# Storing the first attention's queries in 2 KB runs, and taking a tile of 32 queries as every fourth column

## The chip, the core and the metric

The kernel runs on one core of one Trainium2 chip, as one launch. Times are device microseconds (us) of that core. The work is spread over TensorE (PE in the profile; its weight loads are PEld), VectorE (DVE), ScalarE (ACT), GpSimd (POOL), the issuing queue of SyncE (SP) and 16 DMA engines. Lower is better.

## What is computed

One encoder layer over 2048 tokens with 1024 features, in float32. Cut to what matters here:

```python
h  = rms_norm(x) * norm_mix
q_a, k_a, v_a, q_b, k_b, v_b, g_a, g_b = split(h @ w_in)     # 512 128 128 512 512 512 1024 1024
y_a = windowed_gqa(q_a, k_a, v_a, sink)      # 8 query heads in 2 groups of 4, 64 wide, one K and V per group
y_b = neighborhood_attn(q_b, k_b, v_b, rpb)  # 8 heads on a 32 x 64 grid of tokens
x  = x + (sigmoid(g_a + b) * (y_a @ w_proj_a) + sigmoid(g_b + b) * (y_b @ w_proj_b)) @ w_out
x  = x + relu(rms_norm(x) @ w_up) ** 2 @ w_down
out = rms_norm(x) * norm_final

# windowed_gqa, for a block of 128 queries and the 384 keys around it
sc = (q . k) * 64 ** -0.5 - slope[head] * |t - s|      # only where |t - s| <= 128
p  = softmax over the keys and one more logit, sink[head]
y  = p @ v
```

## The kernel before

**Precision.** Every operand of a large product is held as a high part (rounded to the format that TensorE reads in one pass) and a low part (the remainder); the product is three matmuls, high x high, high x low and low x high. So each result that becomes an operand again is written twice: ScalarE writes the high part, VectorE the low one.

**Stages.** First stage (about the first 360 us): the input projection for token blocks 0 and 1 (512 tokens each), and for most columns in a scheme with seven products in place of eight (`in_quad`, in the order 1, 2, 5, 6, 7, 4, 3). Its results go through `in_result`. Then the kernel runs the first attention (`attn_a`, 32 units: 2 head groups by 16 blocks of 128 tokens, about 360 to 615 us), and between its instructions, as filler, the same projection for token blocks 2 and 3 (`qk_tile`, `v_tile`, `gate_tile`). The second attention follows with more filler, then the output projection, and the two layers of the feed-forward part, which take the larger half of the time.

**Where queries come from.** A slice is one tile of 128 features (two heads) by one block of 512 tokens. `qk_parts` writes a slice's high and low parts side by side into a tile `t2` and returns the pairs of places for the DMAs that store it in DRAM. The query columns are `O_QA` to `O_KA`: four tiles of features, four blocks, 16 slices. The store is `qs_a[g][m]`, for head group `g` and half `m` of the tokens; its 128 rows are the 64 high and 64 low features of a head. Eight slices are made in the first stage (tile `ze`, a ring of two buffers, stored at L468), eight during the attention (tile `z`, a ring of three, stored at L709). The lines in question before: L446 (ScalarE) and L447 (VectorE) write the two parts with the scale 1/8 applied. The key and query tiles of the second attention take the other branch, L442 and L443, in which key tiles are written in steps of four words and query tiles in reversed runs of adjacent words.

**How `attn_a` uses them.** A unit loads its queries with one DMA (L774) into a tile `qa` with three buffers. It works in four steps of 32 tokens: the 32 queries of four heads are the 128 columns of the stationary operand (L784), and the 288 keys around them are the moving operand, in two matmuls (the high and low keys against the high and low queries, then crosswise). Before, a step's 128 columns are adjacent in the tile:

```python
PE.matmul(ps[:, :n], q[:, u].rearrange("p h q -> p (h q)"), ka[:, z, base + lo : base + hi], ...)
```

VectorE adds the bias of the distances and takes the row maximum (L786), ScalarE makes the exponentials (L788 to L791), GpSimd divides (L795), TensorE transposes (L802), the transposed part is split by ScalarE and VectorE (L805, L806), and two matmuls a chunk make the output (L807, L808); L813 and L814 evict it.

**Order.** Nothing in the code fixes the order of all instructions: a planner places them, engine by engine, by its own costs, with a few bounds written out by hand (`issue_after`). SP issues nearly all DMAs in one queue, in order; ScalarE issues a few.

Of the kernel before, what the change touches and what calls it, by code (L numbers as in the profile page):

```python
# [8 lines left out]
F32 = mybir.dt.float32  # L9
F32R = mybir.dt.float32r  # L10
AF = mybir.ActivationFunctionType
ALU = mybir.AluOpType
# [10 lines left out]
P = 128  # L23
KC = D // P
NB = 4
BT = 512
# [4 lines left out]
A_Q = 32  # L31
# [3 lines left out]
O_QA, O_KA, O_VA, O_QB, O_KB, O_VB, O_GA, O_GB = 0, 512, 640, 768, 1280, 1792, 2304, 3328  # L35
# [60 lines left out]
def encoder_layer(ctx, tc, x, norm_mix, w_in, b_gate, sink, rpb, w_pa, w_pb, w_out,  # L96
                  norm_mlp, w_up, w_down, norm_final, dist_a, mask_b, out):
    nc = tc.nc
    V, A, G, PE, SY = nc.vector, nc.scalar, nc.gpsimd, nc.tensor, nc.sync
# [16 lines left out]
    dp = pool("dp", space=DRAM)  # L116
# [10 lines left out]
    def T(pl, shape, dt, tag, bufs):  # L127
        n_t[0] += 1
        pl = pl[tag] if isinstance(pl, dict) else pl
        return pl.tile(shape, dt, tag=tag, bufs=bufs, name=f"{tag}_{n_t[0]}")  # L130
# [20 lines left out]

    qs_a = [[dp.tile([P, 32, 4, A_Q], F32, name=f"qs_a{g}{m}") for m in range(2)] for g in range(2)]
    ks_a = [dp.tile([2, P, S // 2], F32, name=f"ks_a{m}") for m in range(2)]
    vs_a = [dp.tile([2, P, 8, P], F32, name=f"vs_a{m}") for m in range(2)]
    qs_b = [dp.tile([2, P, 4, 4, P], F32, name=f"qs_b{t}") for t in range(4)]
# [225 lines left out]
    last_part, last_low = [None], [None]  # L383
# [45 lines left out]
    def qk_parts(col, b, src, t2):  # L429

        th, tl = t2[:, 0], t2[:, 1]
        if O_QB <= col < O_VB:
            if col < O_KB:

                pv = src.rearrange("p (r j c) -> p j r c", r=8, j=4)
                hv, hr, lr = (flipped(t) for t in (th, th.bitcast(F32R), tl.bitcast(F32R)))
            else:

                pv = src.rearrange("p (q r x) -> p q r x", q=2, r=4)
                hv, hr, lr = (t.rearrange("p (q x r) -> p q r x", q=2, r=4)  # L440
                              for t in (th, th.bitcast(F32R), tl.bitcast(F32R)))
            A.copy(hr, pv)  # L442
            V.tensor_tensor(out=lr, in0=pv, in1=hv, op=ALU.subtract)  # L443
        else:
            scale = 1.0 if col == O_KA else 0.125
            A.activation(th.bitcast(F32R), src, AF.Copy, scale=scale)  # L446
            last_low[0] = V.scalar_tensor_tensor(out=tl.bitcast(F32R), in0=src, scalar=scale, in1=th,  # L447
                                                 op0=ALU.mult, op1=ALU.subtract).ins
        parts = [(e, t2[e * 64 : e * 64 + 64]) for e in range(2)]
        if col < O_KA:  # L450
            dst, h = qs_a[col // 256][b // 2], col // P % 2 * 2
            n = BT // A_Q
            dst = dst.rearrange("(z p) u h q -> p z u h q", z=2)[:, :, b % 2 * n : (b % 2 + 1) * n]
            return [(dst[:, z, :, h + e], t[:, z].rearrange("p (u q) -> p u q", u=n)) for e, t in parts for z in range(2)]
        if O_QB <= col < O_KB:
            dst = qs_b[(col - O_QB) // P]
            return [(dst[e].rearrange("(z p) b j q -> p z b (j q)", z=2)[:, :, b], t) for e, t in parts]
        dst, o = (ks_a[b // 2], b % 2 * BT) if col == O_KA else (ks_b[(col - O_KB) // P], b * BT)
        return [(dst[e].rearrange("(z p) t -> p z t", z=2)[:, :, o : o + BT], t) for e, t in parts]
# [90 lines left out]
    for k in range(KC):  # L550
        ps = zbank(*tbanks[k % 6])
        turned(ps, tiles[0], k)
        h, l = (t[:, k % 4] for t in right[1 + k // 4])
# [142 lines left out]
    h_pages(2)  # L696


    def qk_tile(col, scale, tiled=False):
        raw = load_slice([(cols(w_in[0], col), KC)])  # L700
        yield
        hl = split_slice(raw, V if col == O_KA else G)
        yield
        for b in (2, 3):
            ps = psum("mm", 2)
            feature_tile(ps, hl, hp[b])
            out = qk_parts(col, b, ps, T(wp, [P, 2, BT], F32, "z", 3))
            for dst, t in out:
                SY.dma_start(dst, t)  # L709
            yield  # L710

    def v_tile(col):
        raw = load_slice([(cols(w_in[0], col), KC)])
        yield
        hl = split_slice(raw, V if col == O_VA else G)
        yield
        for b in (2, 3):
            ps = psum("mm", 2)
            feature_tile(ps, hl, hp[b])
            vt = T(wp, [P, 2, BT], F32, "z", 3)[:, 0]  # L720
            A.copy(vt, ps)
            out = v_parts(col, b, vt, psum("mm", 2), T(wp, [P, 2, BT], F32, "z", 3).rearrange("p a b -> p (a b)"))
            for dst, t in out:
                SY.dma_start(dst, t)
            yield
# [3 lines left out]
    SY.dma_start(dist, dist_a)  # L729
    bias_a = [None] * 2  # L730

    by_head = T(ap_, [P, 4], F32, "byhead", 1)
    slope, sink_p = by_head[:, 0:2], by_head[:, 2:4]
    for h in range(4):
        at = slice(h * A_Q, (h + 1) * A_Q)
        for g in range(2):
            G.memset(slope[at, g : g + 1], 2.0 ** -(4 * g + h + 1))
        G.tensor_copy(out=sink_p[at], in_=sink_t[at].rearrange("p (g h) -> p g h", g=2)[:, :, h])

    def make_bias_a(g):  # L740
        t = T(ap_, [P, A_K], F32, f"biasa{g}", 1)
# [23 lines left out]
    def attn_a(g, i):  # L765
        c0, c1 = (1 if i == 0 else 0), (2 if i == 15 else 3)
        if bias_a[g] is None:

            with tc.issue_after(shares[2]):
                make_bias_a(g)  # L770
        base = (i - 1) * P
        q = T(ap_, [P, 4, 4, A_Q], F32R, "qa", 3)
        s = sas[len(began) % 4]
        began.append(SY.dma_start(q.bitcast(F32), qs_a[g][i // 8][:, i % 8 * 4 : i % 8 * 4 + 4]).ins)  # L774
        ka, v = kas[g], vas[g]
        st = T(ap_, [P, 8, 4], F32, "sta", 8)
        mx, nm, sm, es, ri = (st[:, k, :] for k in range(5))
        sink_g = sink_p[:, g : g + 1]
        span = [(max(u * A_Q, c0 * P), min(u * A_Q + A_K, c1 * P)) for u in range(4)]
        for u, (lo, hi) in enumerate(span):  # L780
            n = hi - lo
            ps = psum("s", 3)
            for z in range(2):
                PE.matmul(ps[:, :n], q[:, u].rearrange("p h q -> p (h q)"), ka[:, z, base + lo : base + hi],  # L784
                          start=z == 0, stop=z == 1)
            V.tensor_tensor_reduce(out=s[:, u, lo:hi], in0=ps[:, :n], in1=bias_a[g][:, lo - u * A_Q : hi - u * A_Q],  # L786
                                   scale=1.0, scalar=sink_g, op0=ALU.add, op1=ALU.max, accum_out=mx[:, u : u + 1])
        A.activation(nm, mx, AF.Copy, scale=-1.0)  # L788
        A.activation(es, mx, AF.Exp, bias=sink_g, scale=-1.0)
        for u, (lo, hi) in enumerate(span):  # L790
            A.activation(s[:, u, lo:hi], s[:, u, lo:hi], AF.Exp, bias=nm[:, u : u + 1], accum_out=sm[:, u : u + 1])  # L791
        V.tensor_tensor(out=sm, in0=sm, in1=es, op=ALU.add)
        V.reciprocal(ri, sm)
        for u, (lo, hi) in enumerate(span):
            share = G.tensor_scalar(s[:, u, lo:hi], s[:, u, lo:hi], ri[:, u : u + 1], 1.0, ALU.mult, ALU.mult)  # L795
        shares.append(share.ins)
        yield
        po = psum("av", 1)
        for c in range(c0, c1):
            pt = psum("pt", 2)  # L800
            for u in range(4):
                PE.transpose(pt[:, u * P : (u + 1) * P], s[:, u, c * P : (c + 1) * P], ident)  # L802
            ph = T(ap_, [P, 512], F32R, "ph", 3)
            pl = T(ap_, [P, 512], F32R, "pl", 3)
            A.copy(ph, pt)  # L805
            V.tensor_tensor(out=pl, in0=pt, in1=ph.bitcast(F32), op=ALU.subtract)  # L806
            PE.matmul(po, v[:, i - 1 + c, :], ph, start=c == c0, stop=False)  # L807
            last = PE.matmul(po, v[:, i - 1 + c, :], pl, start=False, stop=c == c1 - 1).ins  # L808
        done.append(last)
        t = T(ap_, [64, 512], F32, "ya", 2)  # L810
        t4 = t.rearrange("d (h u q) -> d h u q", h=4, u=4)
        by_u = po.rearrange("p (u h q) -> p h u q", u=4, h=4)
        A.copy(t4, by_u[64:128])  # L813
        V.tensor_tensor(out=t4, in0=by_u[0:64], in1=t4, op=ALU.add)  # L814
        flush(queue=SY)
        put(y_a[g].rearrange("(h d) t -> d h t", d=64)[:, :, i * P : (i + 1) * P],
            t.rearrange("d (h q) -> d h q", h=4))
# [38 lines left out]
            yield  # L856


    dense = [qk_tile(O_KA, 1.0), v_tile(O_VA)]
    dense += [qk_tile(O_QA + t * P, 0.125) for t in range(4)]  # L860
    for t in range(4):
        dense.append(qk_tile(O_KB + t * P, 0.125))
        dense.append(qk_tile(O_QB + t * P, 1.0, tiled=True))
        dense.append(v_tile(O_VB + t * P))
    dense += [gate_tile(f, (2, 3)) for f in range(16)]
    for n in (0, 0, 1):
# [789 lines left out]
```

## Time and profile before

| | |
|---|---|
| median of three runs | 2615.67 us (2615.21 to 2619.52) |
| the profiled execution | 2615.13 us |
| its span, first to last instruction | 2613.4 us |
| TensorE busy | 2575.6 us, 99% |
| VectorE, ScalarE, GpSimd busy | 1604.9, 1230.9, 348.2 us |
| DMA queue of SP | 396416 packets, 470.99 MB, 57.9% of the 16 engines' span |
| mean granted TensorE clock | 0.998 |

How to read it: a profile is one execution. Busy times are unions of an engine's instructions; matmuls overlap each other in them, since their ends are modelled. In the view of stretches each row is one window of the span (its start and end, its length, then for each engine the busy time and the number of instructions, the granted clock of TensorE, the share of the DMA engines' time and GB/s). In the timeline a row is the start, the length, the engine, the line, the operation, its output and inputs and its count, with the idle time before it and what ended it in brackets. In the list of waits a row is the waiting instruction, what it waited for, the total in us, how often, and the longest. In the groups a row ends with the busy time, the mean length of one in ns, and the idle time of the engine before these instructions.

### The profile page before, as it was taken

The numbers are of one execution on the slowest core, as the hardware profiler recorded it, in microseconds if no ns is written. First come the engines' busy times: TensorE is split into PE (matmuls) and PEld (weight loads), VectorE is DVE, ScalarE is ACT, GpSimd is POOL, SyncE is SP. The second block draws the span as 40 slices with busy tenths as digits, with TensorE's granted clock in tenths as the row PEclk, the third lists the DMA queues.
The fourth block names the chain that finished last, engine by engine and source line by source line (L and its number), as shares of the span: only waits on it lengthen the run. The fifth ranks groups of instructions, "written<-read, shape, count | busy, mean of one in ns | idle before, by whom it ended". The sixth has DMA issues, their size and how long they took to land.

```text
span 2613.4 us, 34714 instructions
## 1 busy us (share of the span) xinstructions
PE 2575.6 (99%) x12140; PEld 2147.1 (82%) x12140; DVE 1604.9 (61%) x2621; ACT 1230.9 (47%) x2261; POOL 348.2 (13%) x461
## 2 busy tenths in 40 slices
PE   7999999999999999999999999999999999999999
PEld 6788788878888888888888888888888888888887
DVE  8776566655544444765578677766656535554766
ACT  5244346665555555633335544644444322322454
POOL 1000113334555551000001000100000000000010
PEclk9999999999999999999999999999999999999999
DMA  6767376565876745964556755854428825445555
GB/s 185 184 167 204 123 247 172 123 181 136 223 219 184 201 144 162 304 191 150 168 191 203 242 211 199 308 185 149 153 97 308 299 97 185 145 146 169 185 193 171
DMA packets 403647, 490.26 MB, mean 188 GB/s; under 512 B 94840, under 2 KB 238328, under 8 KB 401296
## 3 DMA queue, kind: packets, MB, share of 16 engines
q1 hardware_dynamic: 396416, 470.99, 57.9%
q10 hardware_dynamic: 7056, 17.04, 1.8%
q8 instruction: 96, 1.57, 0.2%
q14 instruction: 79, 0.65, 0.1%
HBM read 328.49 MB, written 159.45 MB: 187 GB/s over the span
## 4 chain that ended last, share of the span: by engine, by line
PE 87%; DVE 5%; DMA 3%; ACT 2%; issue 1%; SPq 1%; POOL 0%; DVEq 0%; POOLq 0%; ACTq 0%
PE b L300 15%; PE b L302 15%; PE b L301 15%; PE mm L205 6%; PE mm L203 6%; PE mm L204 6%; PE pt L203 2%; PE pt L204 2%; PE pt L205 2%; PE zb L302 2%; PE av L987 2%; PE zb L300 2%; PE zb L301 2%; PE pt L975 2%; PE s L947 2%; PE pt L802 1%
## 5 line engine op out<-in xcount | busy, mean ns | idle before, releaser
L301 PE MATMUL b<-dwh,dah 128*128 128x512 f32 x896 | 348.5, 389 | 0.0
L302 PE MATMUL b<-dwh,dah 128*128 128x512 f32 x896 | 347.6, 389 | 0.0
L300 PE MATMUL b<-dwh,dah 128*128 128x512 f32 x896 | 339.6, 389 | 0.0
L296 ACT CAST dah<-da 128x1024 fp32r<-128x1024 f32 (+1 forms) x128 | 120.9, 945 | 368.2 <-PE b L302 244.2
L297 DVE TENSOR_TENSOR dah<-da,dah 128x1024 fp32r<-128x1024 f32 (+1 forms) x128 | 139.5, 1090 | 224.1 <-ACT dah L296 224.0
L301 PE MATMUL b<-ubh,uwhlb 128*128 128x512 f32 x592 | 230.3, 389 | 0.0
L300 PE MATMUL b<-ubh,uwhlb 128*128 128x512 f32 x592 | 230.2, 389 | 0.0
L302 PE MATMUL b<-ubh,uwhlb 128*128 128x512 f32 x592 | 229.2, 389 | 0.0
L203 PE MATMUL mm<-hT,whl 128*128 128x512 f32 x544 | 218.9, 402 | 0.0
L205 PE MATMUL mm<-hT,whl 128*128 128x512 f32 x544 | 215.4, 396 | 0.0
L204 PE MATMUL mm<-hT,whl 128*128 128x512 f32 x544 | 214.9, 395 | 0.0
L300 PE MATMUL zb<-zh,zwhl 128*128 128x512 f32 x476 | 187.5, 395 | 10.5 <-DVE zc L293 5.9
L301 PEld LDWEIGHTS b<-dwh,dah 128*128 128x128 f32 x896 | 168.2, 188 | 34.9
L302 PEld LDWEIGHTS b<-dwh,dah 128*128 128x128 f32 x896 | 168.2, 188 | 34.9
L300 PEld LDWEIGHTS b<-dwh,dah 128*128 128x128 f32 x896 | 168.2, 188 | 34.8
L301 PE MATMUL zb<-zh,zwhl 128*128 128x512 f32 x476 | 187.2, 393 | 0.0
L302 PE MATMUL zb<-zh,zwhl 128*128 128x512 f32 x476 | 184.3, 394 | 1.9 <-DVE zwhl L297 1.9
L293 DVE TENSOR_TENSOR uc<-b,uc 128x512 f32<-128x512 f32 x160 | 109.1, 689 | 104.2 <-PE b L302 103.2
L1526 POOL TENSOR_TENSOR st<-st,power 128x1 f32<-128x1 f32 x16 | 13.3, 841 | 924.9 <-DVE st L1525 924.8
L300 PEld LDWEIGHTS b<-ubh,uwhlb 128*128 128x128 f32 x592 | 111.1, 188 | 23.4 <-issue 0.4
L301 PEld LDWEIGHTS b<-ubh,uwhlb 128*128 128x128 f32 x592 | 111.1, 188 | 23.2
L302 PEld LDWEIGHTS b<-ubh,uwhlb 128*128 128x128 f32 x592 | 111.2, 188 | 23.0
(253 smaller groups left out, 5819.9 us busy)
## 6 DMA issues: line engine op xcount, KB each, us to landing
at<-uc SPq DMA_DIRECT2D x224, 256.0 KB
da<-at SPq DMA_DIRECT2D x96, 512.0 KB
dw<-in_w_down_dram SPq DMA_DIRECT2D x160, 256.0 KB
uraw<-in_w_up_dram SPq DMA_DIRECT2D x32, 1024.0 KB
raw<-in_w_in_dram SPq DMA_DIRECT2D x34, 512.0 KB
zraw<-in_w_in_dram SPq DMA_DIRECT2D x16, 1024.0 KB
z<-zg SPq DMA_DIRECT2D x64, 256.0 KB
qa<-qs_a SPq DMA_DIRECT2D x32, 256.0 KB
```

What stands on the lines that cost most here:

```text
L203: PE.matmul(ps, lh, rh, start=first, stop=False)
L204: PE.matmul(ps, lh, rl, start=False, stop=False)
L205: PE.matmul(ps, ll, rh, start=False, stop=last)
L293: return eng.tensor_tensor(out=out, in0=a, in1=b, op=op).ins
L296: A.copy(hi, src)
L297: return eng.tensor_tensor(out=lo, in0=src, in1=hi.bitcast(F32), op=ALU.subtract).ins
L300: PE.matmul(ps, lh, rh, start=first, stop=False, skip_group_check=True)
L301: PE.matmul(ps, lh, rl, start=False, stop=False, skip_group_check=True)
L302: PE.matmul(ps, ll, rh, start=False, stop=last, skip_group_check=True)
L947: PE.matmul(ps[:, :n], q[:, i, :], kv[:, z, B_R0[i] // 4 : (B_R0[i] + B_NR[i]) // 4, 4 * B_C0[j] : 4 * (B_C0[j] + w)], start=z == 0, stop= ...
L975: PE.transpose(pt[:kp, at + (i - i0) * P : at + (i - i0 + 1) * P], s[i][:, rr : rr + kp], ident)
L987: last = PE.matmul(po[:, i0 * P : (i0 + ni) * P], v[:kp, c, :], src[:kp, o : o + ni * P], start=first, stop=(c == 7 and z == 1), skip_grou ...
```

## The change

The store `qs_a` loses its order by steps of 32 queries: a head's 128 tokens of a block now lie together, and the four blocks of 128 tokens of a slice follow each other, so a slice is stored in runs of 512 words (2 KB) by two DMAs instead of four DMAs with runs of 32 words. To keep the rows of a step together in the result, a block's tokens are written permuted: token `u * 32 + q` goes to place `q * 4 + u`. This is done where the parts are written, by the access patterns of ScalarE and VectorE. The load of a unit reads four runs of 128 words for each row instead of one run of 512, and the stationary operand of step `u` is every fourth column from `u` on.

The scale 1/8 leaves the queries: scores are eight times as large, so slopes and the sink in the running maximum are multiplied by eight, and the three ScalarE instructions after it carry the factor 0.125. Queries, keys and the rest of the branch are now written by a plain copy and a subtraction. The names `scale` and `tiled` of `qk_tile` go, which nothing used.

```diff
-    qs_a = [[dp.tile([P, 32, 4, A_Q], F32, name=f"qs_a{g}{m}") for m in range(2)] for g in range(2)]
+    qs_a = [[dp.tile([P, 4, 8, P], F32, name=f"qs_a{g}{m}") for m in range(2)] for g in range(2)]
...
-            scale = 1.0 if col == O_KA else 0.125
-            A.activation(th.bitcast(F32R), src, AF.Copy, scale=scale)
-            last_low[0] = V.scalar_tensor_tensor(out=tl.bitcast(F32R), in0=src, scalar=scale, in1=th,
-                                                 op0=ALU.mult, op1=ALU.subtract).ins
+            pv, hv, hr, lr = src, th, th.bitcast(F32R), tl.bitcast(F32R)
+            if col < O_KA:
+                pv = src.rearrange("p (i u q) -> p i u q", u=4, q=A_Q)
+                hv, hr, lr = (t.rearrange("p (i q u) -> p i u q", u=4, q=A_Q) for t in (hv, hr, lr))
+            A.copy(hr, pv)
+            last_low[0] = V.tensor_tensor(out=lr, in0=pv, in1=hv, op=ALU.subtract).ins
...
-            n = BT // A_Q
-            dst = dst.rearrange("(z p) u h q -> p z u h q", z=2)[:, :, b % 2 * n : (b % 2 + 1) * n]
-            return [(dst[:, z, :, h + e], t[:, z].rearrange("p (u q) -> p u q", u=n)) for e, t in parts for z in range(2)]
+            dst = dst.rearrange("(z p) h i q -> p z h (i q)", z=2)
+            return [(dst[:, :, h + e, b % 2 * BT : (b % 2 + 1) * BT], t) for e, t in parts]
...
-            G.memset(slope[at, g : g + 1], 2.0 ** -(4 * g + h + 1))
+            G.memset(slope[at, g : g + 1], 2.0 ** (2 - 4 * g - h))
...
+    G.tensor_scalar(sink8, sink_p, 8.0, 1.0, ALU.mult, ALU.mult)
...
-        q = T(ap_, [P, 4, 4, A_Q], F32R, "qa", 3)
+        q = T(ap_, [P, 4, P], F32R, "qa", 3)
...
-        began.append(SY.dma_start(q.bitcast(F32), qs_a[g][i // 8][:, i % 8 * 4 : i % 8 * 4 + 4]).ins)
+        began.append(SY.dma_start(q.bitcast(F32), qs_a[g][i // 8][:, :, i % 8]).ins)
...
-                PE.matmul(ps[:, :n], q[:, u].rearrange("p h q -> p (h q)"), ka[:, z, base + lo : base + hi],
+                PE.matmul(ps[:, :n], q.rearrange("p h (q u) -> p u (h q)", u=4)[:, u], ka[:, z, base + lo : base + hi],
...
-                                   scale=1.0, scalar=sink_g, op0=ALU.add, op1=ALU.max, accum_out=mx[:, u : u + 1])
-        A.activation(nm, mx, AF.Copy, scale=-1.0)
-        A.activation(es, mx, AF.Exp, bias=sink_g, scale=-1.0)
+                                   scale=1.0, scalar=sink8[:, g : g + 1], op0=ALU.add, op1=ALU.max, accum_out=mx[:, u : u + 1])
+        A.activation(nm, mx, AF.Copy, scale=-0.125)
+        A.activation(es, mx, AF.Exp, bias=sink_g, scale=-0.125)
...
-            A.activation(s[:, u, lo:hi], s[:, u, lo:hi], AF.Exp, bias=nm[:, u : u + 1], accum_out=sm[:, u : u + 1])
+            A.activation(s[:, u, lo:hi], s[:, u, lo:hi], AF.Exp, bias=nm[:, u : u + 1], scale=0.125,
+                         accum_out=sm[:, u : u + 1])
```

More of the change, by code (lines that the diff above doesn't have):

```diff
@@ L696, in encoder_layer, with qk_tile @@
     h_pages(2)
-    def qk_tile(col, scale, tiled=False):
+    def qk_tile(col):
         raw = load_slice([(cols(w_in[0], col), KC)])
@@ L730, in encoder_layer @@
     bias_a = [None] * 2
-    by_head = T(ap_, [P, 4], F32, "byhead", 1)
-    slope, sink_p = by_head[:, 0:2], by_head[:, 2:4]
+    by_head = T(ap_, [P, 6], F32, "byhead", 1)
+    slope, sink_p, sink8 = (by_head[:, n : n + 2] for n in (0, 2, 4))
     for h in range(4):
@@ L856, in gate_tile @@
             yield
-    dense = [qk_tile(O_KA, 1.0), v_tile(O_VA)]
-    dense += [qk_tile(O_QA + t * P, 0.125) for t in range(4)]
+    dense = [qk_tile(O_KA), v_tile(O_VA)]
+    dense += [qk_tile(O_QA + t * P) for t in range(4)]
     for t in range(4):
-        dense.append(qk_tile(O_KB + t * P, 0.125))
-        dense.append(qk_tile(O_QB + t * P, 1.0, tiled=True))
+        dense.append(qk_tile(O_KB + t * P))
+        dense.append(qk_tile(O_QB + t * P))
         dense.append(v_tile(O_VB + t * P))
```

## The prediction, made before the changed kernel was run

> **What bounds the kernel now.** I read the page first, then the stretches (busy time of each engine in chosen windows), the waits, the timeline around the places that touch the first attention's queries, and last the groups by form that price single instructions.
>
> ```profile
> span 2613.4 us, 34714 instructions
> ...
> PE 2575.6 (99%) x12140; PEld 2147.1 (82%) x12140; DVE 1604.9 (61%) x2621; ACT 1230.9 (47%) x2261; POOL 348.2 (13%) x461
> ...
> DMA packets 403647, 490.26 MB, mean 188 GB/s; under 512 B 94840, under 2 KB 238328, under 8 KB 401296
> ```
>
> TensorE is busy for 99% of the span, so an edit shows in the time only if it lengthens what TensorE does or fills one of its few holes. The change touches two stretches: 30 to 130 us, where the first stage computes and stores the queries of token blocks 0 and 1, and 360 to 615 us, where the first attention runs while the queries of blocks 2 and 3 are still being made.
>
> ```profile
> core 0: us, PE busy (x) PEld busy (x) DVE busy (x) ACT busy (x) POOL busy (x), PEclk, DMA share, GB/s
> 30.00:50.00 20.00, 19.60 (x93) 15.93 (x91) 20.00 (x26) 14.63 (x22) 0.00 (x0) 1.00 0.44 76
> 50.00:70.00 20.00, 16.66 (x71) 12.90 (x70) 20.00 (x23) 7.51 (x9) 0.00 (x0) 1.00 0.36 106
> ...
> 90.00:110.00 20.00, 20.00 (x92) 16.60 (x91) 15.69 (x19) 7.73 (x10) 0.00 (x0) 1.00 0.97 223
> 110.00:115.00 5.00, 2.64 (x12) 1.86 (x10) 1.45 (x3) 0.63 (x1) 0.00 (x0) 1.00 0.99 218
> 115.00:120.00 5.00, 4.74 (x14) 3.78 (x15) 3.97 (x7) 1.56 (x2) 0.00 (x0) 0.66 0.98 194
> ...
> 360.00:615.00 255.00, 248.54 (x1335) 206.99 (x1335) 155.03 (x456) 161.90 (x460) 96.16 (x179) 1.00 0.66 171
> ```
>
> Three readings. From 30 to 70 VectorE is busy without a break and TensorE waits for it. From 90 to 120 the DMA engines are full (0.97 to 0.99), and at 110 to 120 TensorE loses time, once to a hole and then to a granted clock of 0.66. From 360 to 615 TensorE is busy 248.5 of 255 us at full clock: that stretch has 6.5 us to spare and no more.
>
> **The stores, and the stall that they cause.** A slice of queries (128 features by 512 tokens) is stored today by four DMAs of 64 x 16 runs of 128 bytes. There are 16 slices, so 64 DMAs and 65,536 runs: over two thirds of the 94,840 packets under 512 B. The change makes it two DMAs a slice, each 64 x 2 runs of 2 KB. What the small runs cost shows here:
>
> ```profile
> ACT ze L446 <- DMA qs_a<-ze: 14.6, 4, 4.4
> ```
>
> ```profile
> 111.80 0.39 PE L300 MATMUL zb<-zh,zwhl 128*128 128x512 f32 x1
> ...
> 112.25 0.39 PE L302 MATMUL zb<-zh,zwhl 128*128 128x512 f32 x1
> 113.16 0.63 ACT L446 ACTIVATE ze<-zc 128x512 fp32r<-128x512 f32 x1 [4.60 <-DMA ks_a<-ze]
> 113.82 0.69 DVE L447 SCALAR_TENSOR_TENSOR ze<-zc,ze 128x512 fp32r<-128x512 f32 x1 [3.55 <-ACT ze L446]
> 114.43 2.01 DVE L293 TENSOR_TENSOR zc<-zb,zc 128x512 f32<-128x512 f32 x3
> 115.26 0.47 PE L300 MATMUL zb<-zh,zwhl 128*128 128x512 f32 x1 [2.62 <-DVE zc L293]
> ...
> 119.90 0.40 PE L301 MATMUL zb<-zh,zwhl 128*128 128x512 f32 x1
> ```
>
> ScalarE waits for one of the two store buffers to drain through the full DMA queues; VectorE's low part (L447) waits for ScalarE; the PSUM additions (L293) are queued behind it on VectorE; and TensorE waits for the bank that they free. Matmuls start 0.225 us apart before the hole (two steps from 111.80 to 112.25). From 112.25 to 119.90 there are 14 steps, which would take 3.2 us and took 7.65: the hole and the slow clock behind it cost 4.5 us. With 2 KB runs I expect this to go whole, since six of the eight slices of this stage are what fills the queues between 80 and 117. What is late next is VectorE, busy 15.7 of 20 us in 90 to 110, with room. **Minus 4.5 us**; between 0 (the wait goes on behind weight loads and block loads on the same queues) and 4.5.
>
> **The evictions.** Each of the 16 slices is now written permuted: VectorE and ScalarE write every fourth word, and VectorE reads the high part back in the same steps. The K tiles of the second attention already do exactly this, and the query tiles of that attention do it with adjacent words. These rows are from 30 to 140 us (first four) and 140 to 180 us (last two):
>
> ```profile
> L447 DVE SCALAR_TENSOR_TENSOR ze<-zc,ze 128x512 fp32r<-128x512 f32 x7 | 4.8, 689 | 10.0 <-ACT ze L446 10.0
> L446 ACT ACTIVATE ze<-zc 128x512 fp32r<-128x512 f32 x7 | 4.4, 632 | 21.4 <-DMA qs_a<-ze 14.6 <-DMA ks_a<-ze 4.6 <-DVE zc L293 2.2
> L443 DVE TENSOR_TENSOR ze<-zc,ze 128x512 fp32r<-128x512 f32 x6 | 4.1, 691 | 7.4 <-ACT ze L442 7.4
> L442 ACT CAST ze<-zc 128x512 fp32r<-128x512 f32 x6 | 3.7, 620 | 15.8 <-DMA qs_a<-ze 9.0 <-DMA qs_b<-ze 6.7
> ```
>
> ```profile
> L442 ACT CAST ze<-zc 128x512 fp32r<-128x512 f32 x6 | 6.7, 1115 | 9.6 <-DVE zc L293 7.9 <-DMA ks_b<-ze 1.7
> L443 DVE TENSOR_TENSOR ze<-zc,ze 128x512 fp32r<-128x512 f32 x6 | 6.6, 1106 | 4.2 <-ACT ze L442 4.0
> ```
>
> Dropping the scale changes nothing (689 against 691, 632 against 620 ns). The step of four words adds 0.5 us on ScalarE and 0.4 us on VectorE a slice. Six of the first stage's eight slices and all eight of the second lie where VectorE has idle time, so TensorE covers them; without that cover each would cost 0.4 to 0.9. Two slices are evicted near 38 to 40 us, in the stretch where VectorE has none, and TensorE then waits for VectorE to the end of it:
>
> ```profile
> 66.06 0.50 PE L302 MATMUL zb<-zh,zwhl 128*128 128x512 f32 x1 [1.45 <-DVE zwhl L297]
> ```
>
> **Plus 0.9 us** (two times 0.4, rounded up; 0 to 1.8, the upper end if ScalarE's share comes on top).
>
> **The query loads.** A tile of queries becomes 128 x 4 runs of 512 bytes, where it was one run of 2 KB a partition. The second attention's query load has this very shape, and its store the shape of the new store:
>
> ```profile
> L468 SPq DMA_DIRECT2D qs_a<-ze x32: 574/764/4041, 37.6 to 117.0; - x32
> L774 SPq DMA_DIRECT2D qa<-qs_a x32: 319/326/1609, 356.8 to 594.6; - x32
> ...
> L934 SPq DMA_DIRECT2D qb<-qs_b x32: 521/556/1768, 547.0 to 958.0; - x32
> ...
> L709 SPq DMA_DIRECT2D qs_b<-z x16: 574/605/837, 529.2 to 727.1; - x16
> ```
>
> On SP's queue 32 loads grow by 0.23 us each (+7.4), and 32 stores of about 0.6 to 0.76 go (-19 or more), so the loads of weights behind them in that queue start no later. Three buffers hold the tiles, a unit of attention lasts 8 us (255 us for 32), and neither here nor with the second attention's loads does TensorE wait for one. **Zero**; without that cover each tile would come later by the 0.23 us of its longer issue, 7 us in all.
>
> **The weight loads: the term that decides.** TensorE takes the queries as the stationary operand. Today a tile's 128 columns are adjacent words; after the change they lie 16 bytes apart. There are 256 such loads, all in the attention. No load of this kind is in the trace, so I bound it.
>
> ```profile
> L784 PEld LDWEIGHTS s<-ka,qa x256: 186/188/193, 366.9 to 613.5; 128*128 128x128 f32 x128
> L784 PE MATMUL s<-ka,qa x256: 234/295/407, 367.1 to 613.6; 128*128 128x288 f32 x112, 128*128 128x160 f32 x4, 128*128 128x192 f32 x4, 128*128 128x224 f32 x4
> ```
>
> ```profile
> 366.87 0.86 PEld L784 LDWEIGHTS s<-ka,qa 128*128 128x128 f32 x6
> ...
> 367.09 0.82 PE L784 MATMUL s<-ka,qa 128*128 128x160 f32 x6
> ...
> 455.58 0.95 PE L784 MATMUL s<-ka,qa 128*128 128x288 f32 x6
> ...
> 459.37 0.60 PE L802 MATMUL pt<-ident,sa 128*128 128x128 f32 x4
> ...
> 613.43 0.43 PE L784 MATMUL s<-ka,qa 128*128 128x160 f32 x2
> ```
>
> Six matmuls of only 160 to 224 columns take 0.82 us, the last some 0.28 of it, so 0.108 us apart: here the next load sets the pace, for fewer columns do not go faster. At 288 columns they are (0.95 - 0.295) / 5 = 0.131 us apart: a load of 0.108 is hidden, with 0.023 to spare. How long is a load with a step of 16 bytes? The same step costs ScalarE (1115 - 620) / 512 = 0.97 ns a word and VectorE (1106 - 691) / 512 = 0.81. On 128 columns that is 0.10 to 0.12 us more: 0.212 to 0.232, and I take 0.222. The lower end is a load that keeps 0.108 us and costs nothing; a gain is excluded, since the same columns and words are loaded. The upper end is the load's whole 0.188 us times ScalarE's 1.8 (1115 / 620), 0.34.
>
> In the timeline, from the run at 367.09 to the one at 613.43, 177 of the 256 follow another matmul of the kind: 119 of these start at most 0.14 us after it, 39 from there to 0.23, 19 later. 28 follow a transpose (0.11 apart: 0.60 less the last one's 0.27, over three), 51 a matmul of 512 columns, whose 0.225 hides a load of 0.222. So: 119 x (0.222 - 0.131) = 10.8; about 1 for the 39; 28 x (0.222 - 0.11) = 3.1; together **plus 15 us** (0 to 42). Some of the 6.5 us in which TensorE now waits for softmax work in this stretch is covered by it: **minus 1.5**.
>
> The Trainium skill speaks against the change here: "Advanced Engine Details and Errata", section SBUF Cachelines, has SBUF read in lines of 16 bytes and wants two hits on a line to hide its access. At a step of four words each line is hit once. It gives no time for a weight load; the rows of ScalarE and VectorE above agree with it, and no row of TensorE shows it.
>
> **The sum.** The profiled execution took 2615.1 us (span 2613.4, some 1.7 around it), 0.5 below the median of three. 2615.7 - 4.5 + 0.9 + 15 - 1.5 = **2625.6 us**. The scale that moves into the exponential, one small operation for the sink and the other constants are instructions that exist now or a single one on GpSimd, which is busy for 13%: nothing.
>
> **Rivals.**
> - *The strided load stays hidden.* For it: a load has 0.131 us before it shows, and it lasts 0.108 now; TensorE may fetch a line for each column without loss. Against it: the two other engines both pay. Then 2615.7 - 4.5 + 0.9 = 2612.1, not slower. It decides from below a load of some 0.15 us, where the cost (about 119 x 0.02 + 28 x 0.04 = 3.5) eats the gain. By the Trainium skill, "TensorE: Matmul & The Clock Gate", section LDWEIGHTS, a load's time goes by its columns alone (128 / 1.2 = 107 ns), which would be this rival; the trace agrees with the figure for adjacent words and does not show another step.
> - *The stall stays.* If weights and token blocks fill the DMA queues alone, the store buffers drain as late as now and the 4.5 us are not won: 2630.1. Against it: the queues are at 0.36 from 50 to 70, when none of these stores is under way.
> - *The load is priced by its whole duration*, 0.34 us: then the 51 behind wide matmuls pay too, and the time is 2612.1 + 42 - 1.5, about 2653.
>
> **How the numbers follow.** Forecast 0.57, hidden load 0.28, stall stays 0.10, dear load 0.05. A planner orders the instructions by its own costs, and other costs may order them otherwise; TensorE's idle time now (2613.4 - 2575.6 = 37.8 us) is what that could grow or shrink, and I allow 4 us either way. 0.2% is 5.2 us, about what a measurement of this kernel can tell from no change. Faster by more: half of the hidden case, 0.14. Within: the rest of that case, and the forecast's low end (a load of 0.18 us costs 8), 0.22. Slower: 0.64. The forecast's own range is 2618 to 2630; the whole, 2609 to 2633, leaves out the dear load and the tails.
>
> **What would show it.** In the changed profile: matmuls of L784's kind in runs of six taking about 1.4 us where they take 0.95 (right), or 0.95 still (wrong, and the time then 2612); no wait of ScalarE for the query stores and no hole near 115 us; query evictions at 1.1 us on both engines; TensorE's hole at 66 us, or those before it, longer by up to 1 us; no wait of TensorE for the query loads. A new wait on DMA in the attention, or a hole elsewhere in the first 130 us, would make the sum wrong.

## The result, and the profile after

| | median us (lowest to highest) | against the kernel before, 95% interval |
|---|---|---|
| before | 2615.78 (2613.10 to 2619.52) | |
| after | 2624.57 (2623.51 to 2625.74) | 1.0032 (1.0019 to 1.0045) |

The change is slower by 0.32%, 8.8 us between the medians; 2625.6 was forecast. The page of the profile after; its execution took 2623.5 us:

```profile
span 2621.7 us, 34638 instructions
...
PE 2590.6 (99%) x12140; PEld 2169.9 (83%) x12140; DVE 1612.6 (62%) x2621; ACT 1238.5 (47%) x2261; POOL 347.7 (13%) x462
...
DMA packets 353984, 490.26 MB, mean 187 GB/s; under 512 B 28793, under 2 KB 188665, under 8 KB 351633
```

The small packets went (94,840 to 28,793 under 512 B) and the span grew by 8.3 us. Stretches of the profile after, in the columns of the prediction's table (the number behind an x counts every instruction that lies at least in part in the window):

```profile
110.00:115.00 5.00, 5.00 (x23) 4.14 (x23) 3.77 (x6) 1.64 (x2) 0.00 (x0) 1.00 0.83 270
115.00:120.00 5.00, 5.00 (x23) 4.13 (x23) 2.58 (x5) 1.24 (x2) 0.00 (x0) 1.00 0.71 175
```

Between 110 and 120 us the two rows hold 46 matmuls (23 and 23) where they held 26 (12 and 14) before, at full clock, with the DMA engines at 0.83 and 0.71 instead of 0.99 and 0.98. The stall is gone. Now the first attention. The instructions on its queries, from the first weight load to the last (behind the count: the shortest, median and longest duration in ns, then the first and the last start in us), and the stretch between these two times in either kernel (first the stretch of before, whose instructions the prediction shows, then both of after):

```profile
366.90:613.60 246.70, 240.24 (x1299) 200.10 (x1297) 150.03 (x447) 159.41 (x454) 93.98 (x155) 1.00 0.64 166
```

```profile
L786 PEld LDWEIGHTS s<-ka,qa x256: 307/313/334, 362.6 to 623.4; 128*128 128x128 f32 x128
L786 PE MATMUL s<-ka,qa x256: 239/396/525, 362.8 to 623.5; 128*128 128x288 f32 x112, 128*128 128x160 f32 x4, 128*128 128x192 f32 x4, 128*128 128x224 f32 x4
```

```profile
362.60:623.50 260.90, 256.99 (x1298) 223.77 (x1297) 154.01 (x446) 163.28 (x454) 94.26 (x156) 1.00 0.56 156
```

The same number of matmuls (1299 and 1298) takes 260.9 us instead of 246.7. So the 8.3 us of the span are: 4.3 less up to the attention's first weight load (366.9 to 362.6), 14.2 more in the attention, and 1.6 less behind it. Each of these is one execution against another; what of them belongs to the change is worked out below.

### The profile page after: what moved, and what is told of

The parts are those of the page before. It is cut to its first block, busy times and chain, and to the rows that moved or that the text cites. A ratio compares the mean times of both kernels' runs of the same rounds, so it can differ in the third digit from the quotient of the medians.

```text
span 2621.7 us, 34638 instructions
## 1 busy us (share of the span) xinstructions
PE 2590.6 (99%) x12140; PEld 2169.9 (83%) x12140; DVE 1612.6 (62%) x2621; ACT 1238.5 (47%) x2261; POOL 347.7 (13%) x462
## 2 busy tenths in 40 slices
DMA packets 353984, 490.26 MB, mean 187 GB/s; under 512 B 28793, under 2 KB 188665, under 8 KB 351633
## 3 DMA queue, kind: packets, MB, share of 16 engines
q8 instruction: 96, 1.57, 0.2%
## 4 chain that ended last, share of the span: by engine, by line
PE 89%; DVE 4%; DMA 3%; ACT 2%; issue 1%; SPq 1%; POOL 0%; DVEq 0%; POOLq 0%; ACTq 0%
PE b L300 15%; PE b L301 15%; PE b L302 15%; PE mm L203 6%; PE mm L205 6%; PE mm L204 6%; PE zb L300 3%; PE zb L302 3%; PE zb L301 3%; PE pt L203 2%; PE pt L204 2%; PE pt L205 2%; PE av L990 2%; PE pt L978 2%; PE s L950 2%; PE s L786 2%
```

## The experiments

Theory: the step of 16 bytes between the columns of the stationary operand makes the weight load the pace of these matmuls, and that is nearly all of the cost; the stall is the gain. The rivals: the 512-byte-run loads, the permuted evictions, or another order of instructions make the attention slower. All ratios are to the kernel before, run beside each on the same chip.

The last rival can be met from the traces. Listed in order of start, TensorE's instructions follow each other in the same order in after, e1, e4, e5, e6 and e8 (the runs of the table by their numbers), and in e2 as in before; these two orders differ in 16 of 12,140 places, all within the first 20 us of the attention. e8 below has the order of after and the attention of before, so the order costs nothing.

| run | stores | columns of a step | evictions | attention us | median us | ratio (95%) |
|---|---|---|---|---|---|---|
| before | 128 B | adjacent | plain | 246.6 | 2615.78 | |
| after | 2 KB | 16 bytes apart | step 4 | 260.8 | 2624.57 | 1.0032 (1.0019 to 1.0045) |
| e1_adjacent | 2 KB | adjacent | step 4 | 249.8 | 2612.80 | 0.9991 (0.9982 to 1.0000) |
| e2_step4_before | 128 B | 16 bytes apart | plain | 259.6 | 2627.64 | 1.0047 (1.0035 to 1.0060) |
| e4_plain_evict | 2 KB | 16 bytes apart | plain | 259.6 | 2622.33 | 1.0024 (1.0014 to 1.0034) |
| e5_step2 | 2 KB | 8 bytes apart | step 4 | 249.7 | 2611.75 | 0.9984 (0.9975 to 0.9993) |
| e8_plain_adjacent | 2 KB | adjacent | plain | 246.6 | 2610.50 | 0.9983 (0.9974 to 0.9992) |
| e7_pairs_2loads | 2 KB | 8 bytes apart | step 2 | 248.4 | 2610.43 | 0.9989 (0.9981 to 0.9998) |
| e6_runs256 | 256 B | 8 bytes apart | step 2 | 248.4 | 2609.90 | 0.9979 (0.9971 to 0.9988) |
| e3_gather_load | 2 KB | adjacent | plain | 252.0 | 2612.92 | 0.9992 (0.9983 to 1.0001) |

"Attention" is the time from the first to the last weight load on the queries, from the rows shown below for each run (first and last start).

**Adjacent columns in the changed kernel.**

```diff
-  PE.matmul(ps[:, :n], q.rearrange("p h (q u) -> p u (h q)", u=4)[:, u], ...)
+  PE.matmul(ps[:, :n], q[:, u], ...)
```

> The changed kernel, but step u takes the 128 adjacent columns of head u as its stationary operand (so scores are those of other rows: this leaves the reference). Stores, query loads, permuted evictions and the order of instructions stay. Theory (the step of 16 bytes makes the weight load slow): loads last 0.188 us instead of 0.31, matmuls of this kind start 0.131 us apart instead of 0.233, and the time falls by about 13 us, to 2611 to 2613. Rival (the attention is slower through the 512-byte query loads, the permuted evictions or another order): unchanged, 2623 to 2626.

```profile
L786 PEld LDWEIGHTS s<-ka,qa x256: 186/188/333, 363.2 to 613.0; 128*128 128x128 f32 x128
L786 PE MATMUL s<-ka,qa x256: 234/295/442, 363.4 to 613.1; 128*128 128x288 f32 x112, 128*128 128x160 f32 x4, 128*128 128x192 f32 x4, 128*128 128x224 f32 x4
```

The median load is back at 0.188 us, the attention falls by 11.0 us and the ratio from 1.0032 to 0.9991, about 11 us, with stores, query loads, evictions and order as in the changed kernel. The theory holds. It does not hold for everything: 249.8 is 3.2 us more than before, so something else is longer in the attention too.

**The step of 16 bytes in the kernel before.**

```diff
-  PE.matmul(ps[:, :n], q[:, u].rearrange("p h q -> p (h q)"), ...)
+  PE.matmul(ps[:, :n], q.rearrange("p a h (q u) -> p u (a h q)", u=4)[:, u], ...)
```

> The kernel before, but step u takes every fourth of the tile's 512 words as its stationary operand (other rows: this leaves the reference). Nothing else changes. Theory: the attention grows by 13 to 15 us and the hole near 115 us stays, 2628 to 2631. Rival (the cost comes from what else the change brings): 2615 to 2617.

```profile
L784 PEld LDWEIGHTS s<-ka,qa x256: 307/314/334, 369.8 to 629.4; 128*128 128x128 f32 x128
```

```profile
110.00:120.00 10.00, 7.83 (x28) 6.05 (x27) 5.86 (x9) 2.19 (x3) 0.00 (x0) 0.83 0.98 204
```

This is the cost alone: 0.188 to 0.314 us a load, 246.6 to 259.6 us of attention, 13.0 us, and a time 12 us above before, just under the range expected. The stretch row shows that the stall (28 matmuls in 10 us, clock 0.83, DMA 0.98) is still there: without the new stores it does not go.

**Plain evictions in the changed kernel.**

```diff
-            if col < O_KA:
-                pv = src.rearrange("p (i u q) -> p i u q", u=4, q=A_Q)
-                hv, hr, lr = (t.rearrange("p (i q u) -> p i u q", u=4, q=A_Q) for t in (hv, hr, lr))
```

> The changed kernel, but the query slices are evicted in the order of the tokens, with adjacent words (the rows of a step are then other tokens: this leaves the reference). Theory (evictions cost only in the stretch where VectorE has no idle time, two slices by 0.4 to 0.9 us): faster by 0.9 to 1.5 us, 2623 to 2624, and the attention takes as long as in the changed kernel. Rival (longer evictions also delay the attention through ScalarE and VectorE): faster by 4 us or more, below 2621.

```profile
L783 PEld LDWEIGHTS s<-ka,qa x256: 307/314/334, 360.2 to 619.8; 128*128 128x128 f32 x128
```

The attention takes 1.2 us less than in the changed kernel and exactly what it takes in the run before this one, which has the old stores and loads. The ratio is 0.0008 lower than the changed kernel's, about 2 us; the intervals overlap, so the size of this step is read from the traces alone. Neither expectation holds as it was put: the median lies between the two, and the attention does change, but by little.

**What the other 3.2 us are.** Plain evictions and adjacent columns together:

> The changed kernel with plain evictions and adjacent columns: of the change, the 2 KB stores and the 512-byte-run loads are left (the rows of a step are other tokens and heads: this leaves the reference). With adjacent columns and permuted evictions the stretch from the first to the last query weight load was 249.8 us, against 246.6 in the kernel before; open is what the 3.2 us are. Theory A (the permuted evictions during the attention, through VectorE and ScalarE): 246 to 247 us, and a time of about 2610. Theory B (the query loads in 512-byte runs): still 249 to 250 us, and about 2612.

```profile
L783 PEld LDWEIGHTS s<-ka,qa x256: 186/188/193, 363.1 to 609.7; 128*128 128x128 f32 x128
L773 SPq DMA_DIRECT2D qa<-qs_a x32: 518/557/1193, 351.7 to 590.9; - x32
```

246.6 us, as before, with the 512-byte-run loads in place (0.557 us of issue each): the loads cost nothing, and theory A has the time right. But the 3.2 us are not all waiting. The order of instructions is the same in e1_adjacent and here, so TensorE's waits can be compared one by one. Three waits of e1_adjacent are missing here:

```profile
423.11 1.28 PE L786 MATMUL s<-ka,qa 128*128 128x288 f32 x5 [0.45 <-DVE sta L788]
457.98 0.49 PE L810 MATMUL av<-ph,va 128*128 128x512 f32 x1 [0.47 <-ACT ph L808]
485.60 0.53 PE L786 MATMUL s<-ka,qa 128*128 128x288 f32 x2 [0.89 <-DVE sta L788]
```

Each is for a result of the softmax, and ends 0.2 to 0.5 us after VectorE has written a permuted low part (L450, up to 422.7, 457.8 and 485.1 us). Together they are 1.8 us. The other 1.4 are a slower clock. Both runs wait 2.03 us for VectorE near 490 us, and only in e1_adjacent does the granted clock fall behind it (two rows of e1_adjacent, then two of this run):

```profile
491.20 0.66 PE L805 MATMUL pt<-ident,sa 128*128 128x128 f32 x4 [2.03 <-DVE pl L809]
490.00:500.00 10.00, 8.79 (x42) 7.50 (x43) 6.69 (x18) 6.42 (x17) 1.95 (x4) 0.83 0.48 125
```

```profile
489.40 0.66 PE L802 MATMUL pt<-ident,sa 128*128 128x128 f32 x4 [2.03 <-DVE pl L806]
488.00:498.00 10.00, 8.60 (x48) 7.22 (x49) 7.63 (x23) 7.10 (x20) 1.95 (x4) 1.00 0.48 126
```

The same fall to 0.83 over ten us is in e5_step2, e6_runs256 and e7_pairs_2loads, and neither in the kernel before nor in the changed one. Whether the evictions have a part in it is not shown.

Four runs, with and without the step, with and without permuted evictions, now stand. The step costs 259.6 - 246.6 = 13.0 us with plain evictions and 260.8 - 249.8 = 11.0 with permuted ones, or 12.4 without the slow clock. The evictions cost 1.8 us of waits with adjacent columns and 1.2 with the step.

**A step of 8 bytes.**

```diff
-  PE.matmul(ps[:, :n], q.rearrange("p h (q u) -> p u (h q)", u=4)[:, u], ...)
+  PE.matmul(ps[:, :n], q.rearrange("p (a h) (q w) -> p a w (h q)", a=2, w=2)[:, u // 2, u % 2], ...)
```

> The changed kernel, but the 128 columns of a step lie 8 bytes apart instead of 16 (every second of 256 words: other rows, this leaves the reference). If two words hit in one 16-byte line hide the access: loads at 0.188 us, matmuls 0.131 us apart, 2611 to 2613, as with adjacent columns. Rival (any step but adjacent words costs a second access): loads at 0.31 us and 2623 to 2626. Between them, a load of some 0.16 us in pace: 2616 to 2618.

```profile
L786 PEld LDWEIGHTS s<-ka,qa x256: 192/196/333, 363.2 to 612.9; 128*128 128x128 f32 x128
```

0.196 us, and an attention like that with adjacent columns (249.7 and 249.8). The price sets in between 8 and 16 bytes. "Advanced Engine Details and Errata", section SBUF Cachelines, in the Trainium skill asks for two hits on a line of 16 bytes: for TensorE's weight load the runs agree, 0.188, 0.196 and 0.313 us at steps of 4, 8 and 16 bytes.

**Three versions of the whole computation.** With the step of 8 bytes, runs of 64 words can be formed: tokens are permuted in pairs of steps. One version keeps the 2 KB stores and loads a unit by two DMAs of 256-byte runs; the other stores runs of 256 bytes and loads 2 KB. The third keeps the tokens in order and puts the small runs into the load, four DMAs of 128-byte runs a unit.

```diff
 # pairs, stored in 256-byte runs (e6)
+    qs_a = [[dp.tile([P, 16, 4, 64], F32, name=f"qs_a{g}{m}") for m in range(2)] for g in range(2)]
...
+                pv = src.rearrange("p (i u q) -> p i u q", u=2, q=A_Q)
+                hv, hr, lr = (t.rearrange("p (i q u) -> p i u q", u=2, q=A_Q) for t in (hv, hr, lr))
...
+  PE.matmul(ps[:, :n], q[:, u // 2].rearrange("p h (q w) -> p w (h q)", w=2)[:, u % 2], ...)
...
 # pairs, stored in 2 KB runs, two loads a unit (e7), evictions and columns as in e6
+        for a in range(2):
+            load = SY.dma_start(q[:, a].bitcast(F32), qs_a[g][i // 8][:, :, i % 8, a * 64 : (a + 1) * 64]).ins
...
 # tokens in order, evictions plain, four loads a unit, adjacent columns (e3)
+        for u in range(4):
+            load = SY.dma_start(q[:, u].bitcast(F32), qs_a[g][i // 8][:, :, i % 8, u * A_Q : (u + 1) * A_Q]).ins
```

> The whole computation. Stores in 256-byte runs (four DMAs a slice as before, half as many runs), loads in 2 KB runs as before, tokens permuted in pairs of steps and columns 8 bytes apart. Theory (the stall near 115 us comes from the number of runs): half the runs take the DMA queues below full, the hole is gone or under 1 us, 2610 to 2613. Rival (the stall needs the store to be two DMAs or 2 KB runs): the hole of 2 to 3 us and the slow clock behind it stay, 2614 to 2616.

> The whole computation. Stores in 2 KB runs as in the changed kernel, but tokens permuted only in pairs of steps: a step's columns are every second of 256 words, the evictions write with a step of two words, and a unit's queries are loaded by two DMAs with 256-byte runs, one for each pair of steps. If 8 bytes is free for the evictions as for the weight load (0.69 and 0.62 us a slice), and the second load on SP's queue is covered: no hole near 115 us, attention as before, 2610 to 2612. Rival (evictions in steps of 8 bytes cost as those of 16): 2612 to 2614. If the 32 more loads of about 0.55 us delay the weight loads behind them: above 2615.

> The whole computation. Stores in 2 KB runs with the tokens in order (plain evictions), and the small runs moved to the load: four DMAs of 128-byte runs a unit bring the 128 columns of each step together, so the weight load reads adjacent words. Theory (the loads are issued two units ahead and TensorE does not see them): no hole near 115 us, attention 246 to 247 us, about 2610. Rival (96 more issues of about 0.55 us on SP's queue, 53 us in a stretch of 250, delay the weight and K loads queued behind them): TensorE waits on DMA in the attention, 2616 or more.

The version with 256-byte runs: its weight loads, the evictions of queries between 30 and 140 us (one of the seven is a key slice), and the stretches from 90 to 120 us:

```profile
L786 PEld LDWEIGHTS s<-ka,qa x256: 192/196/333, 362.4 to 610.8; 128*128 128x128 f32 x128
```

```profile
L450 DVE TENSOR_TENSOR ze<-zc,ze 128x512 fp32r<-128x512 f32 x7 | 4.8, 682 | 2.2 <-ACT ze L449 2.2
L449 ACT CAST ze<-zc 128x512 fp32r<-128x512 f32 x7 | 4.6, 659 | 12.1 <-DMA qs_a<-ze 9.3 <-DVE zc L293 2.2 <-DMA ks_a<-ze 0.6
```

```profile
90.00:110.00 20.00, 20.00 (x92) 16.57 (x91) 15.45 (x19) 8.29 (x11) 0.00 (x0) 1.00 1.02 273
110.00:120.00 10.00, 10.00 (x46) 8.29 (x45) 6.55 (x10) 2.19 (x3) 0.00 (x0) 1.00 0.79 212
```

Evictions in steps of 8 bytes take as long as plain ones on VectorE (682 ns) and 0.04 us longer on ScalarE (659). The attention takes 248.4 us, 1.8 more than before; about 1.4 of them are the slow clock behind the wait near 490 us. Halving the number of runs is enough to end the stall: 46 matmuls in 10 us, full clock. It does so without what the theory named: the DMA engines are still full from 90 to 110 us (1.02), and ScalarE still waits 9.3 us for the query stores, but TensorE no longer waits behind it. At 0.9979 it is faster than both kernels. The version with 2 KB stores and two loads is faster too (2610.43 us, as expected, with the same 248.4 us of attention); whether it is behind e6_runs256 the intervals do not tell.

```profile
L788 PEld LDWEIGHTS s<-ka,qa x256: 192/196/333, 361.2 to 609.6; 128*128 128x128 f32 x128
```

With four loads a unit the ratio's interval reaches 1, and the loads are no longer hidden throughout. The waits on the query tile, and the issues:

```profile
L785 PEld LDWEIGHTS s<-ka,qa x256: 186/188/331, 361.4 to 613.4; 128*128 128x128 f32 x128
...
L774 SPq DMA_DIRECT2D qa<-qs_a x128: 518/628/2216, 350.9 to 596.0; - x128
...
  PE s L785: 4.6, 1
```

TensorE waits once, 4.6 us, for a query load. The attention of 252.0 us, against 246.6 with one load a unit, is 5.4 more; 4.6 of them are this wait, and the granted clock is 0.83 in the ten us around its end (392 to 402). The delay that was feared is there, as one wait; the time, 2612.92 us against 2610.50 with one load a unit, lies between the two that were expected.

## Why the prediction was right, step by step

- **The stall: minus 4.5 forecast; held.** TensorE's lost work between 110 and 120 us is back (46 matmuls in the two rows for 26). From the start of the 401st matmul to that of the 501st, which are the same in all runs, it takes 27.15 us before and 26.63 in e2_step4_before, and 22.67 in each of the eight kernels that store in longer runs: 4.5 us less. So it is the number of runs that a store is cut into, as argued: with the old stores the stall stays, with 256-byte or 2 KB runs it goes, whatever the evictions and columns are. It is not another order: up to 130 us e6_runs256 has that of the kernel before on TensorE, VectorE and ScalarE. One sign did not come out. ScalarE still waits for the query stores in the profile after, 6.1 us in this row (30 to 140 us); it is TensorE that does not wait behind it any more:

```profile
L449 ACT CAST ze<-zc 128x512 fp32r<-128x512 f32 x7 | 7.3, 1044 | 11.4 <-DMA qs_a<-ze 6.1 <-DVE zc L293 3.3 <-DVE ze L450 1.2
```

- **The evictions: plus 0.9, and nothing in the attention; half right.** The price of one holds. In the profile after, those on PSUM in the first stage (first two rows) and those in the attention (last two):

```profile
L449 ACT CAST ze<-zb 128x512 fp32r<-128x512 f32 x2 | 2.3, 1155 | 0.0
L450 DVE TENSOR_TENSOR ze<-zb,ze 128x512 fp32r<-128x512 f32 x2 | 2.2, 1091 | 0.0
```

```profile
L450 DVE TENSOR_TENSOR z<-mm,z 128x512 fp32r<-128x512 f32 x8 | 8.9, 1109 | 5.6 <-ACT z L449 5.5
L449 ACT CAST z<-mm 128x512 fp32r<-128x512 f32 x8 | 8.8, 1098 | 5.8 <-PE mm L205 5.8
```

  The early cost shows as longer holes of TensorE behind VectorE, 0.38 to 0.79 us at 39 and 1.56 to 1.98 at 52 us, 0.8 together (two rows of before, then two of after):

```profile
39.20 0.50 PE L300 MATMUL zb<-zh,zwhl 128*128 128x512 f32 x1 [0.38 <-DVE ze L447]
...
52.40 0.47 PE L300 MATMUL zb<-zh,zwhl 128*128 128x512 f32 x1 [1.56 <-DVE zh L525]
```

```profile
38.86 0.50 PE L300 MATMUL zb<-zh,zwhl 128*128 128x512 f32 x1 [0.79 <-DVE ze L450]
...
52.47 0.47 PE L300 MATMUL zb<-zh,zwhl 128*128 128x512 f32 x1 [1.98 <-DVE zh L526]
```

  With plain evictions (e4_plain_evict) they are 0.38 and 1.57 again. The hole at 66 us, 1.45 before, is not in the profile after: the granted clock is 0.91 there from 50 to 70 us, and TensorE runs slower where it waited before.

  What failed is the word "covered" for the eight in the attention. VectorE has idle time there on average (155 of 255 us busy), but a TensorE with 6.5 us to spare waits for single results of the softmax, and the rows of e1_adjacent above show three waits that begin to exist behind a longer eviction: 1.8 us with adjacent columns. With the step the attention is 1.2 us longer for the evictions.
- **The query loads: nothing; held** (246.6 us with them in place). The cover is not endless: with four loads a unit TensorE waited once.
- **The weight loads: plus 15, less 1.5 of slack; held.** Forecast was a load of 0.222 us in pace. Six in a row in the profile after:

```profile
375.69 1.49 PEld L786 LDWEIGHTS s<-ka,qa 128*128 128x128 f32 x6
```

  (1.49 - 0.313) / 5 = 0.235 us apart, and the single load went from 0.188 to 0.313: 0.98 ns a word, where ScalarE's row had said 0.97 and VectorE's 0.81. The attention paid 13.0 us for it with everything else as before; forecast was 13.5 after slack.
- **The sum.** 4.3 less, 14.2 more, 1.6 less behind the attention; forecast was 3.6 less, 13.5 more, 0. The 4.3 flatter the change: the profile after is 0.7 us ahead at the 51st matmul (20.5 against 21.2 us), before a changed instruction has run, and 4.5 less with 0.8 more is 3.7. The 14.2 are 13.0 for the weight loads and 1.2 for evictions that had been put at nothing. The 1.6 behind the attention are the granted clock. Both kernels wait once for a key load there, 2.4 and 2.3 us, and only the execution of before has a slow clock behind it (before first, then after):

```profile
670.00:680.00 10.00, 7.65 (x43) 6.86 (x41) 4.92 (x16) 5.91 (x18) 6.41 (x8) 0.83 1.11 329
```

```profile
680.00:690.00 10.00, 7.66 (x50) 6.85 (x49) 5.06 (x16) 7.46 (x23) 7.52 (x9) 1.00 1.13 328
```

  It is no effect of the change: e2_step4_before, in the order of before and with its stores, has a clock of 1.00 there (680 to 690 us), and e1_adjacent has 0.83 (670 to 680). So the mechanism and the main terms were right, and that the total came within 1.1 us (8.8 between the medians, 9.9 forecast) is in part luck: differences between executions are as large as what was off.
- **The rivals.** That the load stays hidden is refuted by its duration and by e1_adjacent: with 128 columns each, the loads last 0.188, 0.196 and 0.313 us at steps of 4, 8 and 16 bytes. That the stall stays, and that the whole duration counts (42 us), are refuted by the stretch rows.

## What to carry to other kernels

Where TensorE is the bound, an access pattern of its operands is priced before a transfer that other engines hide: a step of 16 bytes between words made every weight load 1.7 times as long, and the kernel paid 13 us to win 4.5. Half the step gave the gain without the price, with stores of 256 bytes as with 2 KB, so the longest run that a store can have is not worth any price: the shortest that ends the stall will do. An engine idle for a third of a stretch does not cover an added instruction if the bound engine waits for single results in its queue.

## What was not expected of the hardware

The price of the step has an edge: copying out of the tile `zc`, ScalarE's evictions took 620, 659 and 1115 ns at steps of 4, 8 and 16 bytes and VectorE's 691, 682 and 1106 (the second values with one plain slice of seven in the mean, the third from the prediction's rows), and TensorE's weight load took 188, 196 and 313. Nearly nothing is paid at 8 bytes, and all of it at 16.

The granted clock falls behind holes of TensorE, and the length of the hole does not decide it between 1.97 and 2.03 us. It fell behind 2.62 us (before, at 115 us: 0.66 over 5 us, so that the hole cost 4.5 us in all), behind 1.98 (after, at 52 us: 0.91 over 20 us) and behind 2.03 (e1_adjacent, at 491 us: 0.83 over 10 us). It stayed at 1.00 behind 1.97 (e1_adjacent, at 53 us) and 2.03 (e8_plain_adjacent, at 489 us). All three falls come to the same: 0.34 x 5, 0.17 x 10 and 0.09 x 20 are 1.7 to 1.8 us of full clock lost. Such a fall is as large as the smaller effects measured here, so traces of one execution each are compared wait by wait, with the clock beside them.
